# Ordered first transfers, first combinations made from a second load of x, and more projections placed behind the two norms in one decoder step

## The chip, the cores and the metric

The kernel runs on one core of a Trainium2 chip. The metric is the device time of one execution in microseconds (us). Five engines work side by side, each with its own queue of instructions: TensorE (PE; it holds a 128x128 block of weights and streams columns past it), VectorE (DVE), ScalarE (ACT), GpSimd (POOL) and SyncE (SP). SP, ACT and POOL also issue DMA transfers, which wait in the issuing engine's queue like any other instruction. Tables of times count from the start of the profiled span.

## The reference, cut to what matters

One layer of a hybrid decoder, for 1024 prompt tokens and 8 sample tokens (T = 1032) of width D = 1024:

```python
def swiglu(x, w1, w3, w2):                 # w1, w3: 1024 x 2816, w2: 2816 x 1024
    return (silu(x @ w1) * (x @ w3)) @ w2

x = layer_norm(ALPHA * x + 0.5 * swiglu(x, ffn1_w1, ffn1_w3, ffn1_w2), ln1_g, ln1_b)
m, states = hybrid_mixer(x, ...)           # RG-LRU branch + gated delta rule (8 heads)
x = layer_norm(ALPHA * x + m, ln2_g, ln2_b)
x = layer_norm(ALPHA * x + 0.5 * swiglu(x, ffn2_w1, ffn2_w3, ffn2_w2), ln3_g, ln3_b)

def hybrid_mixer(x, ...):
    rg_x, rg_y, q, k, v, z, gdn_a, gdn_b, gate_a, gate_b = split(x @ w_in + b_in)
    # RG-LRU: causal conv (4 taps) of rg_x, two block gates, a scan over time
    # gated delta: q, k, v through a causal conv and silu; beta = sigmoid(gdn_b),
    # g = -exp(a_log) * softplus(gdn_a + dt_bias); chunks of tokens with a
    # triangular solve per chunk and a state that is carried from chunk to chunk
    return merged @ w_o, new_state
```

Everything is fp32; the new states of the sample tokens are outputs too.

## The kernel before, in words

**Precision.** Each fp32 operand of a matmul is split in a high and a low part (`split`, L86 to L89 and L91 as the profile names them: a copy on ACT, then a subtraction on DVE). `mm3` multiplies high by high, high by low and low by high, so one projection of 128 output columns for one chunk of tokens is 8 x 3 = 24 matmuls of 128x344. `XH`, `XL` hold the two parts of the layer's input for all tokens, `wh`, `wl` (four buffers each) the two parts of half a weight block (four blocks of 128x128). A weight block first lands in one of three buffers `wraw`.

**Chunks.** The tokens are in three chunks of 344 (`ts(t)`), called c0, c1, c2 here. Each layer norm works by chunk: a sum over the columns, subtraction of the mean, a sum of squares, the scale (`mu`, `rs`), then eight pairs of `ACC`, `XH`, `XL`. The subtractions for `XL` of three of the eight row blocks are on POOL.

**A feed-forward layer** (`ffn`, n = 1 and 2) has 22 units `f` of 128 hidden columns. A *plain* unit is 144 matmuls of 128x344: for each chunk `p1` (w1) and `p3` (w3), then silu and product (`lnq`), stored to DRAM as `gs`. A *Strassen* unit does the same with seven products instead of eight, 168 matmuls of 128x258; it needs the *combinations* `CH`, `CL` of the input, which `combos` makes once in each layer: 16 sums `XH + XL` of 128x516 on POOL (into buffers `G`, `u2`, `si`), 16 additions on DVE, 16 splits (ACT, then DVE). In both layers units f = 0 and 1 are plain, f = 2 to 20 are Strassen, and the combinations are made during f = 1. Unit 21 and w2 follow. In layer 2 the last steps of the norm before it (`fin`) are called from f = 0, and `states` (16 jobs for the sample tokens' states: each loads `s0` and `rb` on POOL's queue, scales on ACT, adds on DVE and stores from ACT's queue, in three steps) is stepped from the units.

**Start.** Unit 0 of layer 1 loads its own x: c0 in eight pieces `ACC<-x` on ACT's queue, c1 and c2 on SP's queue among the weights; the scheduler of the program settled the order in each queue. Constants are loaded on POOL's queue.

**The mixer's beginning** (`kqv_first`): projections K and Q of head 0, `kq(t, i)`, placed around the last steps of LN1; `ab(t)`, 16 matmuls that give the gates' inputs; transposes (L707, L708), the gates' chain of some 25 small operations on DVE that ends with `GG` and `BETA`; and V of head 0, 72 matmuls. Then `gdn(0)` starts from `GG`: factors `gu` on POOL, `kt`, `lt`, a triangular solve `X` of 28 steps on DVE, two passages through DRAM (`d<-lt`, `BL<-d`, and `d<-X`, `IC<-d`), then the matmuls of L848. Projections of the RG branch (`ps_mm` from `wh`, all L130) are placed between these by the scheduler, which sets a fixed order on each engine when the program is built.

## Time and profile before

| what | value |
|---|---|
| time, median of 3 runs | 2636.21 us (2635.96 to 2637.09) |
| the profiled execution | 2637.03 us |
| its span | 2635.1 us |
| granted TensorE clock, mean | 0.984 |
| PE busy | 2535.4 us (96%) |
| DVE busy | 1784.2 us (68%) |
| ACT busy | 1133.9 us (43%) |
| POOL busy | 493.8 us (19%) |

The profiled execution took 1.9 us more than its span and 0.8 us more than the median of the runs. In the tables by window each row gives the stretch, its length, the busy time and count of PE, PEld (the weight loads), DVE, ACT and POOL, the granted clock (1.00 is full), the share of the DMA engines and GB/s. In the timeline a row gives start, length, engine, line, operation, output and inputs, the count, and in brackets the idle time of the engine before it and what ended it. ACTq and SPq are the DMA instructions in those engines' queues.

### The profile page before, as it was taken

To read this page: it belongs to the slowest core of one execution; us is meant where nothing else is said; L and a number is where in the kernel's file an instruction comes from. 1 tells how busy PE (TensorE), PEld (TensorE's weight loads), DVE (VectorE), ACT (ScalarE), POOL (GpSimd) and SP (SyncE) were. 2 spreads that over 40 slices of the span, in tenths; PEclk is the share of its full clock that TensorE was granted. 3 is DMA by queue.
4 is the path that set the end of the run, shared out by engine and by line. 5 is a ranking of instruction groups with operands and counts; after the bars stand their busy time and mean duration, and the time that the engine had idled before them with its cause. 6 is when DMAs were issued, how large, how long until landed. Compare 5 with 4: busy or idle time off the path is not lost.

```text
span 2635.1 us, 47251 instructions
## 1 busy us (share of the span) xinstructions
PE 2535.4 (96%) x18398; PEld 2486.9 (94%) x18398; DVE 1784.2 (68%) x3657; ACT 1133.9 (43%) x2419; POOL 493.8 (19%) x612
## 2 busy tenths in 40 slices
PE   7999999999989999999999999999699999999996
PEld 7999999999979999999999999989699999999996
DVE  7766665645589676777767686767786666666446
ACT  4433333312363737465564637634533333332125
POOL 5000000300332021111112021144521111021013
PEclk8999999999989999999999999999899999999998
DMA  4222222423101121111211121123314444333221
GB/s 140 78 77 82 80 76 70 125 79 113 41 26 51 34 56 43 39 48 34 57 37 53 34 56 36 52 87 117 83 66 112 118 123 119 93 112 110 81 69 65
DMA packets 146816, 195.98 MB, mean 74 GB/s; under 512 B 34720, under 2 KB 75680, under 8 KB 146592
## 3 DMA queue, kind: packets, MB, share of 16 engines
q1 hardware_dynamic: 125024, 154.13, 19.3%
q0 software_dynamic: 10160, 32.06, 4.7%
q10 hardware_dynamic: 11408, 6.77, 0.9%
q8 instruction: 145, 2.38, 0.4%
q14 instruction: 79, 0.65, 0.1%
HBM read 156.15 MB, written 36.76 MB: 73 GB/s over the span
## 4 chain that ended last, share of the span: by engine, by line
PE 80%; DVE 9%; ACT 7%; issue 2%; POOL 1%; DMA 1%; ACTq 0%; SPq 0%; POOLq 0%; DVEq 0%
PE ps_mm L130 32%; PE ps_g L130 11%; PE ps_g L287 10%; PE ps_mm L287 10%; PE ps_sq L287 8%; ACT L88 2%; DVE ACC L94 2%; PE ps_g L848 2%; PE ps_sq L734 2%; DVE ACC L91 1%; ACT lnq L88 1%; DVE wl L91 1%; PE ps_g L734 1%; PE ps_g L740 1%; DMA ACC<-x 1%
## 5 line engine op out<-in xcount | busy, mean ns | idle before, releaser
L130 PE MATMUL ps_mm<-XH,wh 128*128 128x344 f32 x1680 | 568.9, 339 | 11.0 <-ACT XH L88 7.0
L130 PE MATMUL ps_mm<-XL,wh 128*128 128x344 f32 x1680 | 542.2, 323 | 6.2 <-POOL XL L91 6.1
L130 PE MATMUL ps_mm<-XH,wl 128*128 128x344 f32 x1680 | 542.7, 323 | 4.6 <-DVE wl L91 4.6
L88 ACT ACTIVATE wh<-wraw 128x512 fp32r<-128x512 f32 (+2 forms) x366 | 217.8, 599 | 423.2 <-PE ps_mm L130 155.4
L130 PEld LDWEIGHTS ps_mm<-XH,wh 128*128 128x128 f32 x1680 | 320.6, 191 | 15.3 <-ACT XH L88 7.6
L130 PEld LDWEIGHTS ps_mm<-XL,wh 128*128 128x128 f32 x1680 | 320.7, 191 | 8.9 <-POOL XL L91 6.9
L130 PEld LDWEIGHTS ps_mm<-XH,wl 128*128 128x128 f32 x1680 | 320.0, 190 | 5.7 <-DVE wl L91 5.6
L91 DVE TENSOR_TENSOR wl<-wraw,wh 128x512 fp32r<-128x512 f32 (+3 forms) x345 | 246.4, 718 | 52.5 <-ACT wh L88 47.4
L287 PE MATMUL ps_g<-CH,wh 128*128 128x258 f32 x760 | 214.7, 283 | 0.0
L287 PE MATMUL ps_g<-CH,wl 128*128 128x258 f32 x760 | 214.6, 282 | 0.0
L287 PE MATMUL ps_g<-CL,wh 128*128 128x258 f32 x760 | 214.3, 282 | 0.0
L88 ACT ACTIVATE wh<-S 128x512 fp32r<-128x512 f32 x152 | 95.8, 631 | 201.0 <-PE ps_sq L287 129.3
L287 PE MATMUL ps_mm<-XH,wl 128*128 128x258 f32 x608 | 171.5, 282 | 0.7 <-DVE wl L91 0.7
L287 PE MATMUL ps_mm<-XH,wh 128*128 128x258 f32 x608 | 171.8, 282 | 0.5 <-ACT wh L88 0.5
L287 PE MATMUL ps_mm<-XL,wh 128*128 128x258 f32 x608 | 171.3, 282 | 0.0
L342 POOL DMA_DIRECT2D gs<-G x76 | 41.5, 546 | 666.1 <-DVE G L91 618.9
L91 DVE TENSOR_TENSOR wl<-S,wh 128x512 fp32r<-128x512 f32 x152 | 105.0, 691 | 69.4 <-ACT wh L88 69.0
L287 PEld LDWEIGHTS ps_g<-CL,wh 128*128 128x128 f32 x760 | 143.5, 189 | 0.0
L287 PEld LDWEIGHTS ps_g<-CH,wh 128*128 128x128 f32 x760 | 143.2, 188 | 0.0
L287 PEld LDWEIGHTS ps_g<-CH,wl 128*128 128x128 f32 x760 | 143.1, 188 | 0.0
L88 ACT ACT_TABLE_LOAD x109 | 139.8, 1283 | 6.1 <-issue 3.3
L130 PE MATMUL ps_g<-gl,wh 128*128 128x344 f32 x444 | 142.1, 320 | 0.0
(503 smaller groups left out, 6872.5 us busy)
## 6 DMA issues: line engine op xcount, KB each, us to landing
wraw<-w SPq DMA_DIRECT2D x164, 256.0 KB, 2.8
wraw<-w_in SPq DMA_DIRECT2D x128, 256.0 KB, 2.6
gr<-gs SPq DMA_DIRECT2D x84, 258.0 KB, 2.8
gs<-G POOLq DMA_DIRECT2D x76, 258.0 KB, 2.6
wr<-w SPq DMA_DIRECT2D x76, 256.0 KB, 2.6
wraw<-w_o SPq DMA_DIRECT2D x40, 256.0 KB, 2.7
y<-ACC SPq DMA_DIRECT2D x32, 129.0 KB, 1.9
d<-lt SPq DMA_DIRECT2D x8, 512.0 KB, 3.3
```

The costliest lines, as they stand in the source:

```text
L88: return S.activation(out, in_, f, **kw)
L91: return (eng or V).tensor_tensor(out, a, b, op=op)
L94: return V.scalar_tensor_tensor(out, a, s, b, op0=op0, op1=op1)
L130: PE.matmul(p, a, b, start=(n == 0), stop=(n == 3 * nk - 1))
L287: PE.matmul(ps_[c], a[:, k, :], b, start=(start and n == 0), stop=(n == 11), skip_group_check=not start)
L342: G.dma_start(gs[f][:, s], x)
L734: x = PE.matmul(ck(p, i), a, b, start=True, stop=True)
L740: x = PE.transpose(ck(p, i), a, IDT)
L848: pin(PE.matmul(o[r, c, :], a(c), b(c), start=True, stop=True))
```

## The change

It has five parts.

1. *Start.* The pieces of x c0 are issued first, alternately on ACT's and POOL's queue; the four weight blocks of f = 0 are the first four on SP's queue, where w3's go into buffers `wr`, so that they need no free `wraw`; all loads of c1 and c2 follow in one row. These are fixed in this order.
2. *Combinations of layer 1.* The 16 sums on POOL are replaced by 16 loads of the same part of x from DRAM, on SP's queue for half of them and on POOL's for the rest.
3. *V of head 0* is held in four tiles (`hM`, `hP`, `hLT`, `hP2`; names `wv`) and computed for c0 and c1 before `ab(0)`, and for c2 after `kq(2, 1)`, ahead of the transposes.
4. *Layer 2* has three plain units, one Strassen unit less. Order: f = 0 for c0, c1; f = 1 for c0, c1, with its w1 held in other buffers (`rb`, `s0`, `wr`, `S`; names `w1rb` and so on); f = 0 for c2; f = 1 for c2; f = 2 whole; Strassen from f = 3.
5. *`states`* is stepped in layer 2 from the Strassen units alone; what is left is done behind them.

```diff
@@ -25 +25 @@
 LN_EPS = 1e-5
 RMS_EPS = 1e-6
 NF = 22
-FIRST, LASTF = 2, 21
+FIRST, LASTF = {1: 2, 2: 3}, 21
 GROUPS = [[21, 0, 1], [2, 3, 4], [5, 6, 7, 8], [9, 10, 11, 12], [13, 14, 15, 16], [17, 18, 19, 20]]
 TH_ = T // 2
 TQ = T // 4
@@ -105 +105 @@
 
     LNB = {"s1": 3, "mu": 1, "s2": 2, "lnq": 3}
 
-    def wload(src, nk, m=128, eng=None, hold=None):
+    def wload(src, nk, m=128, eng=None, hold=None, raws=None, pin=False):
         hl = []
         for k0 in range(0, nk, 4):
             n = min(4, nk - k0)
             pad = [128, 512 // m, m]
-            raw = wp.tile([128, n, m], F32, name="wraw", tag="wraw", bufs=3, padded_shape=pad)
+            raw = raws() if raws else wp.tile([128, n, m], F32, name="wraw", tag="wraw", bufs=3, padded_shape=pad)
             if hold:
                 h, l = hold(n)
             else:
                 h = wp.tile([128, n, m], F32R, name="wh", tag="wh", bufs=4, padded_shape=pad)
                 l = wp.tile([128, n, m], F32R, name="wl", tag="wl", bufs=4, padded_shape=pad)
-            nc.sync.dma_start(raw, src[:, k0:k0 + n])
+            x = nc.sync.dma_start(raw, src[:, k0:k0 + n])
+            if pin:
+                tc.keep_in_program_order(x)
             split(h, l, raw, eng)
             hl += [(h[:, k, :], l[:, k, :]) for k in range(n)]
         return hl
@@ -140 +142 @@
 
     def x_load(t):
         for k in range(KD):
-            (nc.sync if t else nc.scalar).dma_start(ACC[:, k, ts(t)], A["x"][:, k, ts(t)])
+            q = nc.sync if t else (nc.scalar, G)[k % 2]
+            tc.keep_in_program_order(q.dma_start(ACC[:, k, ts(t)], A["x"][:, k, ts(t)]))
+
+    def x_split(t):
+        for k in range(KD):
             split(XH[:, k, ts(t)], XL[:, k, ts(t)], ACC[:, k, ts(t)])
 
     exps = []
@@ -232 +238 @@
         split(h, l, raw)
         return h, l
 
-    def combos(up):
+    def combos(up, x_src):
         CH_ = up.tile([128, 4, 4, TH_], F32R, name="CH")
         CL = big.tile([128, 4, 4, TH_], F32R, name="CL", tag="A")
         yield CH_, CL
@@ -244 +250 @@
             x1a, x1b, x2a, x2b = b
             for x, r, h in ((x2b, k + 4, 1), (x1b, k, 1), (x1a, k, 0), (x2a, k + 4, 0)):
                 c = slice(h * TH_, (h + 1) * TH_)
-                tt(x, XH[:, r, c].bitcast(F32), XL[:, r, c].bitcast(F32), OP.add, G)
+                if x_src is not None:
+                    d = (nc.sync if k < 2 else G).dma_start(x, x_src[:, r, c])
+                    if k < 2:
+                        tc.keep_in_program_order(d)
+                else:
+                    tt(x, XH[:, r, c].bitcast(F32), XL[:, r, c].bitcast(F32), OP.add, G)
             tt(x2b, x2b, x1b, OP.subtract)
             tt(x1b, x1a, x1b, OP.subtract)
             stt(x1a, x2b, -1.0, x1a, OP.mult, OP.subtract)
@@ -341 +352 @@
         def store(f, s, x):
             G.dma_start(gs[f][:, s], x)
 
-        def plain(f, put, after=None):
-            a1 = wload(w1[f], KD)
-            if n == 1 and f == 0:
+        def weights(f, hold=None, raws=None):
+            first = n == 1 and f == 0
+            if first:
                 x_load(0)
-            a3 = wload(w3[f], KD)
-            for t in range(NT):
+            a1 = wload(w1[f], KD, hold=hold, pin=first)
+            if first:
+                x_split(0)
+            return a1, wload(w3[f], KD, hold=hold, raws=raws if first else None, pin=first)
+
+        def plain(f, put, after=None, w=None, chunks=range(NT), raws=None):
+            a1, a3 = w or weights(f, raws=raws)
+            for t in chunks:
                 s = ts(t)
                 if n == 1 and f == 0 and t:
                     x_load(t)
+                    x_split(t)
                 p1 = psum("mm")
                 mm3(p1[:, :TC], a1, xsl(t), KD)
                 if fin and f == 0 and t < 2:
@@ -365 +383 @@
 
         with pool("ffna%d" % n) as up:
             extra = side(up)
-            make = combos(up)
+            make = combos(up, A["x"] if n == 1 else None)
+            spare = ["S"] * 3 + ["wr"] * 3 + ["s0", "rb"]
+
+            def held(n):
+                return [up.tile([128, n, 128], F32R, name="w1" + x, tag=x, bufs=3 if x in ("S", "wr") else 2) for x in (spare.pop(), spare.pop())]
             for f in range(LASTF):
-                if f < FIRST:
-                    def put(s, p1, p3):
+                if f < FIRST[n]:
+                    def put(s, p1, p3, f=f):
                         si = third()
                         act(si, p1, AF.Silu)
                         stt(si, si, -1.0, p3, OP.mult, OP.mult)
@@ -381 +403 @@
                         if f or t == NT - 1:
                             next(make, None)
                     cx = None if f == 0 else cx
-                    plain(f, put, after)
+                    if n == 1 or f > 1:
+                        plain(f, put, after, raws=lambda: up.tile([128, 4, 128], F32, name="wr", tag="wr", bufs=3))
+                    elif f == 0:
+                        first = (weights(0), put)
+                        plain(0, put, None, first[0], range(2))
+                    else:
+                        w = weights(1, hold=held)
+                        plain(1, put, None, w, range(2))
+                        plain(0, first[1], None, first[0], range(2, NT))
+                        cx = next(make)
+                        next(make)
+                        plain(1, put, None, w, range(2, NT))
+                        next(make)
                 else:
                     strassen(f, w1, w3, up, cx, store)
                     for _ in range(NT):
                         next(extra, None)
+            for _ in extra:
+                pass
 
         with pool("ffnb%d" % n) as up:
             ACC = big.tile([128, KD, T], F32, name="ACC", tag="A")
...
@@ -587 +623 @@
             def ck(x, c):
                 return x[:, c * 128:(c + 1) * 128]
 
-            def pre_tile():
-                pre = mp.tile([128, 3 + T], F32, name="pre", tag="pre", bufs=2)
+            def pre_tile(tag="pre"):
+                pre = mp.tile([128, 3 + T], F32, name="pre", tag=tag, bufs=2 if tag == "pre" else 1)
                 G.memset(pre[:, :3], 0.0)
                 return pre
 
@@ -646 +682 @@
 
             def kqv_first():
                 dst = kqv_dst(0)
+                spare = ["hM", "hP", "hLT", "hP2"]
+
+                def hold(n):
+                    return [mp.tile([128, n, 128], F32R, name="wv", tag=spare.pop()) for _ in range(2)]
                 wk, wq = (wload(A["w_in"][b0], KD) for b0 in (KC, QC))
-                evs = [silu_evac(d, pre_tile(), b0) for d, b0 in zip(dst, (KC, QC))]
+                wv = wload(A["w_in"][VC], KD, hold=hold)
+                evs = [silu_evac(d, pre_tile(x), b0) for d, b0, x in zip(dst, (KC, QC, VC), ("pre", "pre", "lt"))]
                 ab = gates_proj()
 
                 def kq(t, i):
                     p = psum("mm")
-                    mm3(p[:, :TC], (wk, wq)[i], xsl(t), KD)
+                    mm3(p[:, :TC], (wk, wq, wv)[i], xsl(t), KD)
                     evs[i][1](t, p[:, :TC])
 
                 kq(0, 0)
@@ -662 +703 @@
                 next(fin)
                 next(fin)
                 kq(1, 1)
+                kq(0, 2)
+                kq(1, 2)
                 ab(0)
                 ab(1)
                 ab(2)
                 kq(2, 0)
                 kq(2, 1)
+                kq(2, 2)
                 gates()
                 for t in range(NT):
                     for e in evs:
                         e[2](t)
-                for _ in proj(VC, silu_evac(dst[2], pre_tile(), VC)[0]):
-                    pass
                 KQV[0] = dst
 
             GG = mp.tile([128, 9, H], F32, name="GG")
...
```

What this does to the engines' queues, at three places. SP's queue from its first instruction, before (`w_1` stands for w1 and w3 of layer 1):

```order
L119 DMA wraw<-w_1 128x512 x3
L143 DMA ACC<-x 128x344 x6
L119 DMA wraw<-w_1 128x512
L143 DMA ACC<-x 128x344 x10
L119 DMA wraw<-w_1 128x512 x3
L261 DMA wr<-w_1 128x512 x3
L119 DMA wraw<-w_1 128x512
```

and after:

```order
L119 DMA wraw<-w_1 128x512 x2
L119 DMA wr<-w_1 128x512 x2
L146 DMA ACC<-x 128x344 x16
L254 DMA G<-x 128x516 x4
L119 DMA wraw<-w_1 128x512 x3
L272 DMA wr<-w_1 128x512 x3
L119 DMA wraw<-w_1 128x512
L254 DMA si<-x 128x516
L254 DMA u_468<-x 128x516
L254 DMA u_467<-x 128x516
L254 DMA si<-x 128x516
L272 DMA wraw<-w_1 128x512 x3
```

All 16 loads of c1 and c2, and four loads of x for the combinations, now stand between the weights of f = 0 and those of f = 1; the last two weights of f = 0 no longer stand behind six and sixteen pieces of x.

POOL's queue from the first store of f = 0, before:

```order
L342 DMA gs<-lnq 128x344
L91 ISA
L91 TENSOR_TENSOR u_468<-XH,XL 128x516
L342 DMA gs<-lnq 128x344
L91 TENSOR_TENSOR G<-XH,XL 128x516 x4
L91 TENSOR_TENSOR si<-XH,XL 128x516
L91 TENSOR_TENSOR u_467<-XH,XL 128x516
L91 TENSOR_TENSOR si<-XH,XL 128x516
L91 TENSOR_TENSOR G<-XH,XL 128x516 x3
L342 DMA gs<-lnq 128x344
```

and after:

```order
L353 DMA gs<-lnq 128x344
L254 DMA G<-x 128x516 x3
L353 DMA gs<-lnq 128x344
L254 DMA G<-x 128x516
L353 DMA gs<-lnq 128x344
L254 DMA si<-x 128x516
L254 DMA u_616<-x 128x516
L254 DMA u_615<-x 128x516
L254 DMA si<-x 128x516
```

The additions are gone from POOL; eight loads of x stand between the stores, so that the fourth load waits for the second chunk's product and the next four for the third's.

PE around the gates of head 0. Before, this is where `GG` is first used:

```order
L130 MATMUL ps_mm_8728<-XH_69,wl_8718 128x344
L130 MATMUL ps_mm_8728<-XH_69,wh_8717 128x344
L130 MATMUL ps_mm_8728<-XL_70,wh_8717 128x344
L724 MATMUL ps_g_8532<-GG_8167,masks_82 128x64 x2
L724 MATMUL ps_g_8532<-GG_8167,ONES_72 128x64
L130 MATMUL ps_mm_8728<-XH_69,wl_8718 128x344
L130 MATMUL ps_mm_8728<-XH_69,wh_8717 128x344
L130 MATMUL ps_mm_8728<-XL_70,wh_8717 128x344
L130 MATMUL ps_mm_8728<-XH_69,wl_8718 128x344
L740 MATMUL ps_g_8738<-masks_82,kq0_8173 128x128 x4
```

and after:

```order
L132 MATMUL ps_mm_8844<-XL_70,wh_8723 128x344
L132 MATMUL ps_mm_8844<-XH_69,wl_8724 128x344
L132 MATMUL ps_mm_8844<-XH_69,wh_8723 128x344
L766 MATMUL ps_g_8624<-GG_8167,masks_82 128x64 x2
L766 MATMUL ps_g_8624<-GG_8167,ONES_72 128x64
L782 MATMUL ps_g_8738<-masks_82,kq0_8173 128x128 x4
L782 MATMUL ps_g_8761<-masks_82,kq0_8173 128x128 x4
L810 MATMUL ps_g_8796<-gu_8706,SLR_83 128x512
L810 MATMUL ps_g_8796<-gu_8707,SLR_83 128x512
L132 MATMUL ps_mm_8844<-XL_70,wh_8723 128x344
```

Row for row, 72 matmuls of V and 70 more of the RG branch now stand ahead of the first use of `GG`, where before there were 77 between the transposes and it. In both programs PE has the same matmuls up to some 220 rows behind this place, and from there to the end of the mixer the same rows in the same order.

DVE in layer 2, where the weights of the first plain unit behind the norm's last chunk are split (`wl`). Before, these are f = 1's:

```order
L94 SCALAR_TENSOR_TENSOR lnq_21009<-lnq_21009,ps_g_20984 128x344
L91 TENSOR_TENSOR G_21072<-G_21072,G_21070 128x516
L91 TENSOR_TENSOR wl_21091<-wraw_21089,wh_21090 128x512
L91 TENSOR_TENSOR G_21070<-G_21069,G_21070 128x516
L91 TENSOR_TENSOR CL_21068<-G_21072,CH_21067 128x516
L94 SCALAR_TENSOR_TENSOR G_21069<-G_21072,G_21069 128x516
L91 TENSOR_TENSOR wl_21097<-wraw_21095,wh_21096 128x512
```

and after, they are f = 2's:

```order
L91 TENSOR_TENSOR CL_21200<-si_21277,CH_21199 128x516
L91 TENSOR_TENSOR G_21374<-G_21373,G_21374 128x516
L91 TENSOR_TENSOR CL_21200<-G_21376,CH_21199 128x516
L91 TENSOR_TENSOR wl_21297<-wraw_21295,wh_21296 128x512
L94 SCALAR_TENSOR_TENSOR G_21373<-G_21376,G_21373 128x516
L91 TENSOR_TENSOR CL_21200<-G_21374,CH_21199 128x516
L91 TENSOR_TENSOR wl_21303<-wraw_21301,wh_21302 128x512
L94 SCALAR_TENSOR_TENSOR G_21375<-G_21373,G_21375 128x516
L91 TENSOR_TENSOR CL_21200<-G_21373,CH_21199 128x516
L91 TENSOR_TENSOR wl_21309<-wraw_21307,wh_21308 128x512
L91 TENSOR_TENSOR CL_21200<-G_21375,CH_21199 128x516
```

Before, one operation of the combinations stood ahead of the first of these; now 18 stand between the norm's last `XL` and it.

More of the change, by code (lines that the diff above doesn't have):

```diff
@@ L569, in full @@
             def full(tag, n=T):
-                return mp.tile([128, n], F32, name=tag, tag=tag, padded_shape=[128, T])
+                return mp.tile([128, n], F32, name=tag, tag=tag, padded_shape=[128, 3 + T if tag == "lt" else T])
             def eight(tag):
@@ L1067, in slots @@
                             x = mp.tile([128, n * TC], F32R, name="m_" + tag, tag=tag, bufs=2 if tag == "pre" else 1,
-                                        padded_shape=[128, 512] if tag[0] == "h" else [128, TC] if n == 1 else [128, 3 + T] if tag == "pre" else [128, T])
+                                        padded_shape=[128, 512] if tag[0] == "h" else [128, TC] if n == 1 else [128, 3 + T] if tag in ("pre", "lt") else [128, T])
                             ap += [x[:, i * TC:(i + 1) * TC] for i in range(n)]
```

## The prediction

> **What bounds the kernel now.** I read the page first, then PE's busy time by stretch, then PE's waits in the three stretches that the change touches, and there the other engines' timeline.
>
> ```profile
> span 2635.1 us, 47251 instructions
> PE 2535.4 (96%) x18398; PEld 2486.9 (94%) x18398; DVE 1784.2 (68%) x3657; ACT 1133.9 (43%) x2419; POOL 493.8 (19%) x612
> ...
> PE 80%; DVE 9%; ACT 7%; issue 2%; POOL 1%; DMA 1%; ACTq 0%; SPq 0%; POOLq 0%; DVEq 0%
> ```
>
> PE is the bound, 80% of the chain that ended last, and the rest is DVE and ACT at a few places. The windows show where:
>
> ```profile
> core 0: us, PE busy (x) PEld busy (x) DVE busy (x) ACT busy (x) POOL busy (x), PEclk, DMA share, GB/s
> ...
> 6.54:23.52 16.98, 12.80 (x48) 11.01 (x49) 8.51 (x19) 9.22 (x20) 1.19 (x3) 0.80 1.01 317
> 23.52:38.59 15.07, 15.07 (x98) 15.07 (x97) 10.61 (x14) 8.53 (x21) 11.22 (x8) 1.00 0.17 65
> 38.59:73.60 35.01, 27.99 (x149) 26.93 (x147) 34.91 (x41) 12.80 (x23) 18.98 (x14) 0.85 0.15 46
> 73.60:93.61 20.01, 20.01 (x166) 20.01 (x167) 15.70 (x41) 8.20 (x18) 1.08 (x2) 1.00 0.29 91
> 741.85:787.46 45.61, 37.79 (x197) 31.73 (x196) 37.75 (x67) 29.17 (x57) 12.82 (x15) 0.85 0.07 24
> 787.46:800.34 12.88, 12.88 (x88) 12.66 (x87) 12.06 (x43) 5.45 (x13) 1.05 (x3) 1.00 0.14 42
> 800.34:843.41 43.07, 43.07 (x291) 42.58 (x290) 39.59 (x102) 18.86 (x62) 15.42 (x19) 1.00 0.23 61
> 1863.67:1944.39 80.72, 57.51 (x292) 54.18 (x293) 70.40 (x88) 39.28 (x71) 42.55 (x37) 0.85 0.22 60
> 1944.39:1964.61 20.22, 20.22 (x170) 20.22 (x169) 14.44 (x27) 6.67 (x13) 1.08 (x2) 1.00 0.27 90
> ```
>
> The second row is layer 1's f = 0 for c1 and c2: 96 matmuls of 128x344 in 15.07 us, 0.157 us each, so 24 take 3.77 us and a plain unit 22.6 us. The last row is a Strassen unit, 20.2 us. The first row is f = 0 for c0: 48 matmuls in 16.98 us that need 7.5. The third is f = 1 and two matmuls of the first Strassen unit: 35.0 us for about 23. In layer 2, f = 0 and 1 take 80.7 us for 45.2. Once a Strassen unit has begun, PE is busy throughout, so each of these stretches shifts everything behind it one for one. The mixer is different, as below.
>
> **The start.**
>
> ```profile
> PE ps_mm L130 <- ACT XH L88: 7.0, 2, 6.5
> PE ps_g L130 <- ACT wh L88: 3.6, 1, 3.6
> PE ps_mm L130 <- DVE wl L91: 3.0, 1, 3.0
> PE ps_g L130 <- DVE wl L91: 2.8, 1, 2.8
> ```
>
> ```profile
> 9.86 0.49 ACT L88 ACTIVATE XH<-ACC 128x344 fp32r<-128x344 f32 x1 [0.51 <-DMA ACC<-x]
> 11.34 3.05 ACTq L143 DMA_DIRECT2D ACC<-x  x3
> 14.43 1.20 ACT L88 ACTIVATE wh<-wraw 128x512 fp32r<-128x512 f32 x2 [4.08 <-DMA ACC<-x]
> ```
>
> ```profile
> GB/s 0 0 41 141 344 402 372 345 362 392 357 288 192 183 88 255 388 397 393 377 378 387 374 343 360 268 266 306 331 341 284 371 361 156 146 119 11 22 0 0
> ```
>
> ACT issues five pieces of c0, and the last three only at 11.34 to 14.39; `wh` of w3 stands behind them, and PE waits 3.6 us for it. The row of GB/s (40 slices of the first 30 us) stands near 370 with a hole around 10 us. After, four weight blocks and eight pieces of x, 4 x 256 KB + 8 x 172 KB = 2.46 MB, are first in all queues: at 370 GB/s 6.6 us, from about 3.0, landing by 10 to 11. ACT then has XH's last pieces and w3's `wh` done near 11.6; p3 of c0 starts near 12 and c0 ends at 16 (estimates from these rows). Bounds: 14 (PE's 7.5 us right behind the first pieces) and 20.5 (only the 3.05 us saved). I take 16.5, since no issue now stands between. Then 15.1 us for c1 and c2; their 2.82 MB need 7.6 us more, so they are in by 19, ahead of PE.
>
> For the combinations, DVE and POOL disturb each other:
>
> ```profile
> 32.74 5.06 POOL L91 TENSOR_TENSOR G<-XH,XL 128x516 f32<-128x516 f32 x4
> 33.64 8.41 DVE L91 TENSOR_TENSOR wl<-wraw,wh 128x512 fp32r<-128x512 f32 x1 [1.80 <-ACT wh L88]
> ```
>
> One `wl` took 8.41 us, its wait through seven POOL sums of 1.27 us each; this is PE's 3.0 us, the 2.8 behind it is the same again, and the clock of 0.85 is the rest. After, there are no POOL sums here. PE comes to f = 1 at 16.5 + 15.1 = 31.6. By then DVE has 24 `XL`, the first four sums and their splits; counted off in its order, f = 1's four `wl` are ready at about 29, 31, 34 and 36, needed at 31.6, 33.5, 35.4 and 37.3. That is tight: the second half of G waits for c1's store on POOL's queue. I leave 3 us of stalls (bounds 0 and 6, what the two waits took). f = 3 then starts at 31.6 + 22.6 + 20.2 + 3 = 77.4 instead of 93.6: **-16 us** (-21 to -10). The 4.2 MB that x is loaded again fall into stretches in which DMA moved 65 and 46 GB/s, so they displace little.
>
> A rule speaks against the first part. The Trainium skill ("Trainium Kernel Development and Optimization", Key Constraints) says that transfers from SP, ACT and POOL share the same 16 engines, and that issuing from several saves only issue time. The trace agrees on the shared rate (370 to 400 GB/s, whichever queues run); by the rule alone only the 3.05 us of issue would go. That is the bound of 20.5 above.
>
> **LN1 and V.**
>
> ```profile
> PE ps_mm L699 <- DVE XL L94: 2.9, 2, 2.2
> PE ps_sq L169 <- DVE s L91: 2.6, 1, 2.6
> ```
>
> V's c0 and c1 (48 matmuls, 7.5 us) cover the 2.9 us wait of `ab(2)`, and most of the slow clock (0.85 of 45.6 us is 6.8 us of lost work). But V's 11.3 us now stand ahead of the transposes: 787.5 + 11.3 less about 9.5 (the wait and most of the clock's loss) = 789.3. What counts is this chain:
>
> ```profile
> 788.21 0.29 DVE L91 TENSOR_TENSOR GT<-ps_g,b_ab 128x128 f32<-128x128 f32 x1 [0.61 <-PE ps_g L708]
> ...
> 800.05 0.22 DVE L94 SCALAR_TENSOR_TENSOR GG<-GG,a_log 128x72 f32<-128x72 f32 x1
> ...
> 838.30 0.37 DVE L808 COPY X<-X 32x256 f32<-32x256 f32 x1
> ...
> 840.78 0.67 SPq L816 DMA_DIRECT2D IC<-d  x1
> ...
> 843.41 0.64 PE L848 MATMUL ps_g<-IC,hLT 128*64 128x16 f32 x8
> ```
>
> From the transposes to `GG` it takes 12 us and from there to `IC` 43 us, with DVE busy 39.6 of 43.1 (window). PE arrives at L848 just when `IC` is there, and from some rows behind this its order is the same in both programs. So the 9 us or so that PE saves at LN1 only become waits in the first 40 us of `gdn(0)`, unless DVE's chain starts earlier or is shorter. It starts 2 us later, and carries about 3 us less of other work (counted in the orders: 46.6 for 49.5 us). I take **-1 us**, -4 if DVE's waits shrink too, +4 if the chain is not shortened and the clock drops.
>
> **Layer 2.**
>
> ```profile
> PE ps_sq L169 <- DVE s L91: 6.7, 1, 6.7
> PE ps_mm L130 <- POOL XL L91: 6.1, 3, 3.2
> PE ps_mm L130 <- ACT wh L88: 4.0, 1, 4.0
> PE ps_g L130 <- DVE wl L91: 3.8, 1, 3.8
> ```
>
> ```profile
> 1881.25 0.40 ACT L88 ACTIVATE s<-s,KE 128x128 f32<-128x128 f32 x1 [4.15 <-DMA s<-S]
> ...
> 1893.70 0.49 ACT L88 ACTIVATE mu<-mu 128x344 f32<-128x344 f32 x1
> ```
>
> ```profile
> 1908.80 5.28 DVE L91 TENSOR_TENSOR G<-G 128x516 f32<-128x516 f32 x1
> ...
> 1918.55 2.97 DVE L91 TENSOR_TENSOR CL<-G,CH 128x516 fp32r<-128x516 f32 x3
> 1921.44 3.44 DVE L91 TENSOR_TENSOR wl<-wraw,wh 128x512 fp32r<-128x512 f32 x2
> ```
>
> The wait of 4.0 stays. The 6.7 us end late because `states` holds ACT's queue until a load of S lands (1881.25), ahead of the mean; with the job moved down, two weight copies stand there instead. I take 2 us earlier (0 to 5): scale ready at 1892.2 instead of 1894.2. From there PE has 2.7 us of c1's p3, then f = 1 for c0, c1 (15.1), f = 0 c2 and f = 1 c2 (15.1): f = 2 at 32.9 behind the scale. The last `XL` comes about 20 behind it (15.5 before, three more POOL sums ahead), needed at 21: the 6.1 us go. What is late next is f = 2's `wl`, behind 18 operations of the combinations: DVE's own work of 10.3 for the norm and 18 x 0.6 to 1.0 (last rows) is 21 to 28, and POOL's ten sums and four `XL` of together 16 us can block it (the 5.28 us). Between 25 and 38 I take 35, nearer the upper, since here both engines are loaded at once; the last `wl` at 44, where PE wants it at 38.6. Stall 5.5 us (0 to 10). f = 2 is 22.6 us, and f = 3 starts at 1892.2 + 32.9 + 5.5 + 22.6 = 1953.2 instead of 1964.6: **-11 us** (-17 to -5). In it is that a plain unit costs 2.4 us more than the Strassen unit it replaces. `states` needs some 52 steps, 18 Strassen units give 54.
>
> **Sum.** -16 - 1 - 11 = -28 against the profiled execution's 2637.0: 2609; that stands 0.8 us above the median, so 2608.
>
> **Rivals.**
> 1. *The weights of the unit behind the combinations are late in both layers*: stalls of 6 and 10 us instead of 3 and 5.5. For it speaks that DVE is 34.9 of 35.0 us busy in f = 1 before; against it that in layer 1 POOL is free. 2608 + 7.5, about 2616. Chance 0.25.
> 2. *The start saves issue time only* (the rule above): c0 ends at 20.5; 2612, and with rival 1, 2620. 0.15.
> 3. *The mixer takes the whole gain of LN1.* If `gdn(0)` has slack that I do not see, 8 us more go: 2600. Against it, DVE's 92%. 0.12.
> 4. *Slower:* the jobs of `states`, all in Strassen units now, hold ACT's queue as at 1881.25. If a unit's `wh` copies stood 4.15 us behind each of 16 jobs and half of it reached PE, that is +33 us, 2641; it decides from 1.8 us for each job on. Against it: in before's Strassen units the same jobs run and PE is busy for all of 20.2 us. 0.03.
> 5. *No difference to measure* (5.3 us, 0.2%, is about the least that can be told from no change): all three terms at their upper bounds and a little more. 0.04.
>
> My forecast has 0.41. The range of 8 in 10 goes from rival 3 with a little more, 2598, to rivals 1 and 2 together, 2622. Faster by over 0.2%: 0.92; same 0.05; slower 0.03.
>
> **What would show it.** Right: the first Strassen matmul (L298) near 57 us; no DVE operation above 2 us between 15 and 55; ps_mm <- XL no longer in LN1's waits, but new PE waits between 790 and 845 (shifted by 16) ahead of `IC`; in layer 2 `wl` as PE's longest wait behind the norm. Wrong: PE waits for x or wraw at f = 1; `IC` more than 4 us off; ACT waiting for `s<-S` in Strassen units.

## The result, and the profile after

The changed kernel takes 2612.01 us (median of 4 runs, 2609.49 to 2612.86), the kernel before on the same chip 2636.65 us (2635.96 to 2637.68). The ratio is 0.9902, with an interval from 0.9887 to 0.9918: 24.6 us less, where 28 were forecast. Line numbers have moved: L132 is the matmul of `mm3` (L130 before), L298 Strassen's (L287), L175 the sums of the layer norm (L169), L890 the matmuls that wait for `IC` (L848).

The head of the page, and the shares of the chain that ended last:

```profile
span 2611.0 us, 47192 instructions
...
PE 2529.6 (97%) x18374; PEld 2484.1 (95%) x18374; DVE 1749.7 (67%) x3641; ACT 1129.4 (43%) x2414; POOL 477.6 (18%) x609
...
PE 83%; ACT 7%; DVE 6%; POOL 1%; issue 1%; DMA 1%; ACTq 0%; SPq 0%; DVEq 0%; POOLq 0%
```

PE has 83% of that chain instead of 80, DVE 6 instead of 9. The windows, cut at the same places of the program as before (c0, c1 and c2 of f = 0, f = 1, a Strassen unit; LN1's last sums to the transposes, to `GG`, to `IC`; layer 2's f = 0 and 1, f = 2, a Strassen unit):

```profile
5.63:17.35 11.72, 11.72 (x48) 10.52 (x49) 8.59 (x18) 9.37 (x21) 3.82 (x8) 1.00 1.04 346
17.35:32.42 15.07, 15.07 (x98) 15.07 (x97) 13.17 (x26) 11.71 (x26) 3.23 (x6) 1.00 0.95 326
32.42:55.04 22.62, 22.62 (x147) 22.62 (x145) 19.41 (x33) 10.56 (x19) 3.77 (x7) 1.00 0.53 177
55.04:75.20 20.16, 20.16 (x169) 20.16 (x169) 13.80 (x37) 7.53 (x16) 1.08 (x2) 1.00 0.21 64
723.44:772.41 48.97, 44.51 (x269) 40.95 (x267) 46.58 (x85) 33.52 (x65) 14.82 (x18) 0.97 0.12 39
772.41:784.17 11.76, 11.76 (x81) 11.70 (x81) 11.13 (x40) 4.79 (x11) 0.29 (x2) 1.00 0.01 1
784.17:827.85 43.68, 39.60 (x251) 37.80 (x250) 34.77 (x97) 17.22 (x59) 12.41 (x19) 0.96 0.22 59
1845.95:1909.53 63.58, 51.72 (x292) 50.05 (x292) 49.91 (x64) 31.55 (x57) 40.72 (x31) 0.89 0.18 50
1909.53:1940.67 31.14, 25.62 (x145) 25.34 (x145) 22.33 (x36) 11.77 (x23) 7.82 (x10) 0.89 0.42 121
1940.67:1960.88 20.21, 20.21 (x170) 20.21 (x170) 12.31 (x22) 5.74 (x11) 1.08 (x2) 1.00 0.21 66
```

In the first four rows PE is busy throughout, and from the second on at the full clock; f = 1 takes 22.6 us, 35.0 before. The 1.00 of the first row is not a reading: the trace has no entry of the clock before 13.4 us. Its 48 matmuls take 11.7 us where 7.5 are needed, because they start 0.29 us apart or more up to 13.2 us, and 0.157 apart behind it. One of each:

```profile
12.59 0.49 PE L132 MATMUL ps_mm<-XH,wl 128*128 128x344 f32 x1
13.74 0.32 PE L132 MATMUL ps_g<-XL,wh 128*128 128x344 f32 x1
```

Ahead of the transposes PE is idle for 4.5 us (48.97 less 44.51), and between `GG` and `IC` for 4.1, where before it was idle for 7.8 and 0. In layer 2, f = 2 takes 31.1 us for 22.6 us of work.

At four places that both programs pass, the trace gives the three terms (starts in the trace, us):

| place | before | after | difference | so this part |
|---|---|---|---|---|
| second Strassen unit of layer 1, f = 3 | 93.61 | 75.20 | -18.4 | start -18.4 |
| first use of head 1's `IC` | 961.81 | 944.42 | -17.4 | mixer +1.0 |
| f = 3 of layer 2 | 1964.61 | 1940.67 | -23.9 | layer 2 -6.5 |
| last matmul | 2624.13 | 2599.90 | -24.2 | the rest -0.3 |

### The profile page after: what moved, and what is told of

It reads as the page before. It is cut to its first block, busy times and chain, and to the rows that moved or that the text cites. A ratio compares the mean times of both kernels' runs of the same rounds, so it can differ in the third digit from the quotient of the medians.

```text
span 2611.0 us, 47192 instructions
## 1 busy us (share of the span) xinstructions
PE 2529.6 (97%) x18374; PEld 2484.1 (95%) x18374; DVE 1749.7 (67%) x3641; ACT 1129.4 (43%) x2414; POOL 477.6 (18%) x609
## 4 chain that ended last, share of the span: by engine, by line
PE 83%; ACT 7%; DVE 6%; POOL 1%; issue 1%; DMA 1%; ACTq 0%; SPq 0%; DVEq 0%; POOLq 0%
PE ps_mm L132 34%; PE ps_g L132 12%; PE ps_g L298 10%; PE ps_mm L298 10%; PE ps_sq L298 8%; ACT L88 2%; PE ps_g L890 2%; DVE ACC L94 2%; PE ps_sq L776 2%; ACT lnq L88 1%; POOL s L91 1%; PE ps_g L776 1%; PE ps_g L782 1%; DVE ACC L91 1%; ACT ACC L88 1%
## 5 line engine op out<-in xcount | busy, mean ns | idle before, releaser
L132 PE MATMUL ps_mm<-XH,wh 128*128 128x344 f32 x1656 | 560.8, 339 | 12.4 <-ACT wh L88 12.4
L132 PE MATMUL ps_mm<-XH,wl 128*128 128x344 f32 x1656 | 535.6, 323 | 3.7 <-DVE wl L91 3.7
L132 PE MATMUL ps_mm<-XL,wh 128*128 128x344 f32 x1656 | 534.5, 323 | 0.0
L132 PEld LDWEIGHTS ps_mm<-XH,wh 128*128 128x128 f32 x1656 | 316.2, 191 | 16.2 <-ACT wh L88 12.9
L132 PEld LDWEIGHTS ps_mm<-XH,wl 128*128 128x128 f32 x1656 | 315.5, 190 | 4.9 <-DVE wl L91 4.6
L132 PEld LDWEIGHTS ps_mm<-XL,wh 128*128 128x128 f32 x1656 | 316.3, 191 | 1.6 <-DVE XL L91 0.6
L91 DVE TENSOR_TENSOR wl<-wraw,wh 128x512 fp32r<-128x512 f32 (+3 forms) x339 | 228.9, 679 | 42.3 <-ACT wh L88 38.2
L298 PE MATMUL ps_g<-CH,wh 128*128 128x258 f32 x740 | 209.0, 282 | 0.0
L298 PE MATMUL ps_g<-CH,wl 128*128 128x258 f32 x740 | 208.9, 282 | 0.0
L298 PE MATMUL ps_g<-CL,wh 128*128 128x258 f32 x740 | 208.7, 282 | 0.0
L298 PE MATMUL ps_mm<-XH,wh 128*128 128x258 f32 x592 | 167.1, 282 | 0.0
L298 PE MATMUL ps_mm<-XH,wl 128*128 128x258 f32 x592 | 166.9, 282 | 0.0
L298 PE MATMUL ps_mm<-XL,wh 128*128 128x258 f32 x592 | 166.8, 282 | 0.0
L132 PE MATMUL ps_g<-gl,wh 128*128 128x344 f32 x444 | 142.1, 320 | 0.0
L132 PE MATMUL ps_mm<-gl,wh 128*128 128x344 f32 x444 | 142.1, 320 | 0.0
L132 PE MATMUL ps_g<-gh,wh 128*128 128x344 f32 x444 | 142.0, 320 | 0.0
L132 PE MATMUL ps_mm<-gh,wh 128*128 128x344 f32 x444 | 142.0, 320 | 0.0
```

The costliest lines, as they stand in the source:

```text
L91: return (eng or V).tensor_tensor(out, a, b, op=op)
L132: PE.matmul(p, a, b, start=(n == 0), stop=(n == 3 * nk - 1))
L298: PE.matmul(ps_[c], a[:, k, :], b, start=(start and n == 0), stop=(n == 11), skip_group_check=not start)
```

## The experiments

Every kernel here is timed against the kernel before on the same chip (2636.9 to 2637.7 us there).

**The start alone.** The changed kernel without parts 2 to 5: POOL's sums stay, V is computed behind the transposes, layer 2 has two plain units in their old order.

```diff
-FIRST, LASTF = {1: 2, 2: 3}, 21
+FIRST, LASTF = {1: 2, 2: 2}, 21
...
-            make = combos(up, A["x"] if n == 1 else None)
+            make = combos(up, None)
...
```

> Part 1 alone (order of the first transfers). If the terms are independent: c0 ends 6.2 us earlier, f = 1 keeps its two waits of 3.0 and 2.8 us and its slow clock, 2636.7 - 6.2 = 2630.5. Rival: the waits in f = 1 end when POOL's sums end, at a time that the start does not move; then f = 1 only waits longer and the gain is 0 to 3 us, 2634 to 2637.

2630.98 us (2629.09 to 2632.08), ratio 0.9974 [0.9963, 0.9985]. c0 ends at 16.98 us instead of 23.52, 6.5 us earlier, but f = 3 only 5.15 us. PE's waits in the first 75 us, and the window of f = 1, of this kernel:

```profile
PE ps_mm L132 <- ACT wh L88: 10.3, 2, 5.6
PE ps_mm L132 <- DVE wl L91: 5.2, 1, 5.2
```

```profile
33.00:68.00 35.00, 25.81 (x143) 25.31 (x144) 33.86 (x43) 14.03 (x25) 15.33 (x13) 0.80 0.19 66
```

The 5.6 us are the first matmul's. The rest, 9.9 us, stands in f = 1, where PE was idle for 7.0 us in the kernel before: its stalls did not go, and they grew by about 3 us.

**The combinations alone.** The kernel before, with the sums on POOL replaced by loads of x in layer 1.

```diff
-                tt(x, XH[:, r, c].bitcast(F32), XL[:, r, c].bitcast(F32), OP.add, G)
+                if x_src is not None:
+                    d = (nc.sync if k < 2 else G).dma_start(x, x_src[:, r, c])
+                else:
+                    tt(x, XH[:, r, c].bitcast(F32), XL[:, r, c].bitcast(F32), OP.add, G)
...
```

> Part 2 alone (x loaded again in place of POOL's sums, with the start as before). If the contention of POOL's sums with DVE is the whole cause of the losses in f = 1: no DVE operation above 2 us, no PE wait in f = 1, 12.2 us less, 2624.5. Rival: the loads, behind 24 pieces of x and on POOL's queue behind the stores, come later than the sums were; PE waits for wl by 3 us or more, and the gain is 6 us or less, 2631 or more.

2624.12 us (2623.23 to 2625.85), ratio 0.9945 [0.9929, 0.9962]. f = 3 comes at 82.17 us, 11.4 earlier, and the window in f = 1 has no idle PE:

```profile
40.00:62.00 22.00, 22.00 (x143) 22.00 (x141) 16.48 (x28) 9.06 (x16) 2.70 (x5) 1.00 0.37 124
```

**Both.** The changed kernel with layer 2 and the mixer as in the first experiment (the same edit of `FIRST`, V back behind the transposes).

> Parts 1 and 2 (start and combinations of layer 1) without parts 3, 4 and 5. If the parts add up, as the landmarks of the two traces say: the first Strassen unit's steady part 18.4 us earlier than before and nothing else, 2636.7 - 18.4 = 2618. If a later stretch gives part of it back (the mixer's chain, DMA at LN1), 2621 or more.

2617.87 us (2615.61 to 2618.81), ratio 0.9921 [0.9907, 0.9936]. 6.1 and 13.0 us alone, 19.3 together: the two add up.

**c0 on one queue.** The eight pieces of c0 all on ACT's queue; nothing else differs from the changed kernel.

```diff
-            q = nc.sync if t else (nc.scalar, G)[k % 2]
+            q = nc.sync if t else nc.scalar
```

> The changed kernel with all eight pieces of c0 issued on ACT's queue, none on POOL's. If the order of issue is what counts and the queues share the same engines: c0 ends within 1 us of the changed kernel (17.35 us), later by at most the issue time of four more pieces on ACT (4 x 0.45 = 1.8 us). If POOL's queue gives bandwidth of its own: c0 ends 3 us or more later. The whole 2612 to 2614.

2619.28 us (2614.84 to 2622.07), ratio 0.9934 [0.9918, 0.9951]. c0 ends at 23.03 us, 5.7 later than in the changed kernel and only 0.5 ahead of the kernel before; 1 to 1.8 later was expected. The whole is 7.3 us slower in the median, but its runs spread over 7 us, and the profiled one is only 2.0 slower than the changed kernel's. The timeline of ACT from its start, first of the changed kernel, then of this one:

```profile
0.74 1.85 ACTq L146 DMA_DIRECT2D ACC<-x  x4
```

```profile
0.73 7.14 ACTq L146 DMA_DIRECT2D ACC<-x  x8
7.91 1.28 ACT L88 ACT_TABLE_LOAD   x1 [7.91 <-DMA wr<-w]
```

Four pieces take ACT 1.85 us to issue, eight take 7.14. In the trace pieces 6, 7 and 8 are issued at 4.23, 5.39 and 7.54 us, each just behind the landing of an earlier transfer: with SP's weights, eight transfers of SP and ACT were on their way each time. Counted from the end of the issue to the landing, SP and ACT together never have more than eight on their way in any trace of this study, and POOL's queue reaches eight of its own beside them. The last piece lands at 13.64 us instead of 10.53, and ACT's copies to `XH` stand behind the issues. PE's first matmul, in the changed kernel and in this one:

```profile
PE ps_mm L132 <- ACT wh L88: 5.6, 1, 5.6
```

```profile
PE ps_mm L132 <- ACT XH L88: 10.8, 1, 10.8
```

It begins 5.2 us later, which is nearly all of the 5.7.

**The mixer without V.** The changed kernel without part 3.

```diff
-                kq(0, 2)
-                kq(1, 2)
...
-                kq(2, 2)
                 gates()
...
+                for _ in proj(VC, silu_evac(dst[2], pre_tile(), VC)[0]):
+                    pass
```

> The changed kernel without part 3 (V again behind the gates). If the chain on DVE from the transposes to IC bounds gdn(0): L890 1.0 to 1.1 us earlier against the start of LN1 and the whole 1 us faster than the changed kernel, 2611. If V's cover is worth what it removes of PE's waits at LN1 (2.9 us and the slow clock, 8 us in all): 2620.

2610.66 us (2609.86 to 2611.25), ratio 0.9895 [0.988, 0.991]: without V ahead of the transposes the kernel is, if anything, a microsecond faster. Part 3, as it stands, brought nothing.

**V's last chunk behind the transposes.**

```diff
-                kq(2, 2)
                 gates()
+                kq(2, 2)
```

> The changed kernel with V's third chunk (24 matmuls, 3.8 us) behind the gates' transposes instead of ahead. If DVE's chain from the transposes to IC bounds: the transposes 3.8 us earlier, IC 2.5 to 3.5 us earlier, the whole about 3 us faster than the changed kernel, 2609. If PE's own work bounds the beginning of gdn(0): nothing, 2612.

2606.14 us (2604.2 to 2607.03), ratio 0.988 [0.9865, 0.9895]: 6 us less than the changed kernel, where 3 were expected. The windows of this kernel, from the sums of c2 to the transposes, to `GG` and to `IC`:

```profile
723.60:767.34 43.74, 40.78 (x244) 37.31 (x243) 42.73 (x78) 31.82 (x62) 17.76 (x16) 0.96 0.10 30
767.34:779.87 12.53, 12.53 (x85) 12.20 (x84) 11.96 (x43) 4.51 (x12) 1.57 (x4) 1.00 0.16 49
779.87:820.73 40.86, 36.99 (x245) 35.45 (x245) 36.55 (x97) 17.60 (x60) 13.01 (x18) 1.00 0.21 53
```

The transposes begin 5.1 us earlier (767.34 for 772.41), `IC` is used 7.1 earlier, and 6.2 are left at the second head (938.23 for 944.42). From `GG` to `IC` it now takes 40.9 us for 43.7. Against the kernel without part 3 this is 4.5 us less: V for c0 and c1 is worth something ahead of the transposes, V for c2 is not.

**The jobs of `states` in other buffers.** In the changed kernel f = 1's eight held tiles leave one of two `rb` and one of two `s0` free, and the first job of `states` can load into these at once. Here they take both of each, so that its loads go out only behind f = 1.

```diff
-            spare = ["S"] * 3 + ["wr"] * 3 + ["s0", "rb"]
+            spare = ["S"] * 2 + ["wr"] * 2 + ["s0"] * 2 + ["rb"] * 2
```

> The changed kernel with f = 1's w1 and w3 of layer 2 held in both buffers of s0 and of rb (and one S and one wr less), so that the first load of the states' jobs comes behind f = 1. If the jam of those two loads with the weights (7.6 us to landing instead of 2.5) delays the mean of LN2: w1wr's copy and the mean 5 us earlier, the wait of 7.0 us falls to 2, the first Strassen unit of layer 2 comes 5 us earlier, 2607. If the weights are slow for another reason, or the wait has another cause: 2612. A loss is possible if the later loads jam the Strassen weights.

2608.11 us (2605.96 to 2611.33), ratio 0.9889 [0.9875, 0.9904]. PE's waits from the norm to f = 2's end, and what ACT does ahead of the mean, in the changed kernel:

```profile
PE ps_sq L175 <- DVE s L91: 7.0, 1, 7.0
PE ps_mm L132 <- ACT wh L88: 6.7, 2, 4.0
PE ps_mm L132 <- DVE wl L91: 3.7, 2, 2.8
```

```profile
1856.30 0.63 ACT L88 ACTIVATE w1rb<-wraw 128x512 fp32r<-128x512 f32 x1
1862.43 0.63 ACT L88 ACTIVATE w1wr<-wraw 128x512 fp32r<-128x512 f32 x1 [5.50 <-DMA wraw<-w]
1862.97 0.44 ACT L88 ACTIVATE mu<-ps_sq 128x344 f32<-128x344 f32 x1
```

and in this one (of the waits only that for the sums):

```profile
PE ps_sq L175 <- DVE s L91: 2.0, 1, 2.0
```

```profile
1856.21 0.63 ACT L88 ACTIVATE w1s<-wraw 128x512 fp32r<-128x512 f32 x1 [0.43 <-DMA wraw<-w]
1857.32 0.46 ACT L88 ACTIVATE mu<-ps_sq 128x344 f32<-128x344 f32 x1 [0.47 <-PE ps_sq L175]
```

In the changed kernel a weight of f = 1 was issued at 1854.83 and landed at 1862.41, 7.6 us, beside `rb` (broadcast from `rtd`) and `s`, which landed at 1862.06 and 1863.22; the two weights before it took 2.5. ACT stood at its copy with the mean queued behind. Without that jam the mean follows the sums at once, and the first Strassen unit begins at 1933.80 us instead of 1940.67; 0.8 us of this lie ahead of layer 2.

**f = 2's weights ahead of the second quarter of the combinations.**

```diff
                         next(make)
+                        w2_ = weights(2, spin=True)
                         plain(1, put, None, w, range(2, NT))
```

`spin` fixes the splits of these weights, and the next operations of the combinations behind them, in the order in which they are written.

> The changed kernel with f = 2's weights of layer 2 split ahead of the second quarter of the combinations, on ACT and DVE. If f = 2 waits only for its place behind the combinations: the two waits (2.7 and 2.8 us) and the slow clock behind them go, f = 2 takes 22.6 us instead of 31.1, the whole 8 us faster, 2604. Rival: the combinations then are late themselves and the first Strassen unit waits for CL; the gain is 0 to 3 us.

2617.21 us (2613.09 to 2621.07), ratio 0.9923 [0.9908, 0.9937]: slower than the changed kernel. PE's two longest waits behind f = 2, in the first Strassen unit (L303 is Strassen's matmul here):

```profile
PE ps_mm L303 <- ACT wh L88: 5.4, 1, 5.4
PE ps_mm L303 <- DVE wl L91: 2.4, 1, 2.4
```

f = 2's stalls are gone (it ends at 1930.7 us, 10 us earlier), and as much is lost one unit later: these 7.8 us, and a slower clock behind them. f = 4 begins at 1961.70 us, 1960.88 in the changed kernel. That accounts for no gain. The profiled execution is 2.5 us slower than the changed kernel's, and the four runs spread over 8 us; why the median is 5 us slower is not settled.

**Two plain units in layer 2**, in the changed kernel's interleaved order.

```diff
-FIRST, LASTF = {1: 2, 2: 3}, 21
+FIRST, LASTF = {1: 2, 2: 2}, 21
...
-                        next(make)
+                        for _ in make:
+                            pass
```

> The changed kernel with two plain units in layer 2 again, in the new order (f = 0 and f = 1 interleaved, Strassen from f = 2). If the combinations on DVE and POOL bound this stretch (their last CL came at 1926 in the changed kernel, PE was through with f = 1 at 1909.5): the first Strassen unit waits for CL until about 1926, f = 3 starts at 1943 to 1946 instead of 1940.7, the whole 3 to 5 us slower than the changed kernel, 2615 to 2617. If the third plain unit only costs its 2.4 us: 2609.6.

2623.68 us (2620.18 to 2625.97), ratio 0.9945 [0.993, 0.996]: 11.7 us slower than with three, where 3 to 5 were expected, though a Strassen unit is 2.4 us shorter. The first Strassen unit waits, for its weights and not for `CL`:

```profile
PE ps_mm L298 <- DVE wl L91: 11.2, 1, 11.2
PE ps_g L298 <- ACT wh L88: 4.0, 1, 4.0
PE ps_mm L298 <- ACT wh L88: 3.1, 1, 3.1
```

**Layer 2's combinations without POOL.** Is it the number of DVE's operations, or POOL's sums that hold them up?

```diff
-            make = combos(up, A["x"] if n == 1 else None)
+            make = combos(up, A["x"])
```

> The changed kernel, but layer 2's combinations are made from loads of x too, instead of POOL's 16 sums of XH and XL. Part of the computation is changed: they are made of the program's input x and not of LN2's output, so only the time is read. Theory (POOL's sums hold up DVE, whose operations take 1.0 to 1.2 us instead of 0.69 in this stretch, and so f = 2's weights are late): DVE's operations on CL and G go back to about 0.69 us, the two waits of 2.8 and 2.7 us in f = 2 go and f = 2 takes 22.6 us instead of 31.1; the first Strassen matmul of layer 2 comes 8 to 10 us earlier, the time is 2602 to 2604. Rival (DVE has too many operations there, POOL or not): DVE's operations are shorter, but f = 2 still waits 3 us or more for wl, and the time falls by at most 3 us, 2609 or more.

2604.86 us (2604.47 to 2605.2), ratio 0.988 [0.9865, 0.9895]. DVE's splits of one group of the combinations in 1876 to 1941 us, first of the changed kernel, then of this one (count, busy time in us, mean in ns):

```profile
L91 DVE TENSOR_TENSOR CL<-G,CH 128x516 fp32r<-128x516 f32 x8 | 8.5, 1095 | 0.0
```

```profile
L91 DVE TENSOR_TENSOR CL<-G,CH 128x516 fp32r<-128x516 f32 x8 | 5.2, 684 | 0.0
```

And the windows from LN2's last sums to f = 3, in the same order:

```profile
1872.76:1940.67 67.91, 62.39 (x363) 61.35 (x363) 53.12 (x68) 28.74 (x51) 36.09 (x30) 0.92 0.23 68
```

```profile
1872.96:1932.18 59.22, 59.22 (x363) 58.74 (x363) 39.47 (x68) 27.71 (x51) 14.28 (x22) 0.96 0.36 113
```

The same 363 matmuls take 8.7 us less, without any idle PE; as many operations of DVE, 68, take 39.5 us instead of 53.1. It was POOL's sums. Two things change with them, though. DVE's operations are shorter, and the loads, of the program's x in place of LN2's output, wait for nothing in the norm (what layer 2 computes is changed): six operations of the combinations, 4 us of DVE, ran ahead of LN2's scale here (1872.8 to 1877.0). f = 2's first `wl` came 16.1 us earlier (1898.79 for 1914.89), so the head start is the smaller part by this count, but no run separates the two. In layer 1 too the loads need no `XH` and `XL`.

**The same with two plain units.**

> The changed kernel with two plain units in layer 2 instead of three, in the same interleaved order, and layer 2's combinations made from loads of x (of the program's input, not of LN2's output: part of the computation is changed, and only the time is read). With POOL's sums this variant took 2623.7 and its first Strassen unit waited 11.2 us for wl. Theory (POOL's sums hold up DVE): without them two plain units are enough, as they are in layer 1; the 11.2 us go, and the time is 2600 to 2606. Rival (DVE's own operations and the norm don't fit in two units): the first Strassen unit still waits 5 us or more, 2612 to 2620.

2612.41 us (2610.81 to 2615.59), ratio 0.9907 [0.989, 0.9923]. Against 2623.68 with POOL's sums this is 11.3 us less, and the 11.2 us for `wl` are gone; a wait of 5.4 for `wh` is left in the first Strassen unit, and the time falls in the rival's range, but not for the rival's reason. The timeline of ACT:

```profile
1909.15 0.46 ACT L88 ACTIVATE lnq<-ps_mm 128x344 f32<-128x344 f32 x1 [1.49 <-PE ps_mm L132]
1917.43 0.98 ACT L88 ACTIVATE s<-s,KE 128x128 f32<-128x128 f32 x3 [7.82 <-DMA s<-S]
1920.46 0.63 ACT L88 ACTIVATE wh<-S 128x512 fp32r<-128x512 f32 x1 [2.04 <-DVE S L91]
```

ACT is not loaded but waits at the first job of `states`, whose load of S was issued beside the unit's own weights (`rb` took 7.3 us, S 8.4, three weights 7.3 to 8.3). These weights landed at 1916.3 to 1918.4 us, so by these times `wh` could have come little earlier without the job's own wait: what counts is that all of them landed late.

**V late and the jobs late**: the two edits above that gained, together.

> Both of the last two runs' gains together: V's third chunk behind the transposes, and the states' first loads behind f = 1 of layer 2. If they add up: 6 us at gdn(0) and 5 us at LN2 less than the changed kernel, 2601. If one takes the other's gain (LN2's wait is set by something that comes with the mixer): 2605 or more.

2603.07 us (2601.87 to 2605.07), ratio 0.9869 [0.9853, 0.9886]. The two gains, 5.9 and 3.9 us against the changed kernel, come to 8.9 together. This is the fastest kernel of the study.

## Why the prediction came out right

Direction, bound and place were right. That the sum came within 3.4 us is partly luck: the start gave 2.4 us more than forecast, which made up a third of what the mixer (2.0) and layer 2 (4.9) fell short. By its steps:

- **The start** (-16 forecast, -18.4 measured). The two halves were each shown alone. c0 ended at 17.35, forecast 16.5; the lower bound of 14 was out of reach here, since it counts 7.5 us for 48 matmuls, of which the first 22 came 0.29 us apart or more. The term that was mis-sized is "I leave 3 us of stalls": f = 1 took 22.62 us with no wait, so f = 3 came at 75.2 and not at 77.4. The rows say why there was room. The group of f = 1's `wl` splits and one of the combinations' splits (DVE, 15 to 60 us), before and then after:

```profile
L91 DVE TENSOR_TENSOR wl<-wraw,wh 128x512 fp32r<-128x512 f32 x6 | 14.0, 2355 | 5.1 <-ACT wh L88 5.1
L91 DVE TENSOR_TENSOR CL<-G,CH 128x516 fp32r<-128x516 f32 x4 | 4.4, 1129 | 0.0
```

```profile
L91 DVE TENSOR_TENSOR CL<-G,CH 128x516 fp32r<-128x516 f32 x8 | 5.3, 689 | 0.3 <-ACT CH L88 0.3
L91 DVE TENSOR_TENSOR wl<-wraw,wh 128x512 fp32r<-128x512 f32 x6 | 4.1, 685 | 1.2 <-ACT wh L88 1.2
```

  Six splits in 4.1 us instead of 14.0, none slow: "no DVE operation above 2 us" held.
- **The rule against the start** (rival 2, c0 at 20.5) did not hold as it was used: it priced the issue at 3.05 us. The Trainium skill ("Trainium Kernel Development and Optimization", Key Constraints) has several queues save issue time only. c0 from ACT's queue alone was 5.7 us later than from two. The bandwidth is shared, as it says (346 GB/s in c0's window from three queues); but the issue itself waits for earlier transfers, and holds the engine that has to split what has landed.
- **The mixer** (-1 forecast, +1.0 measured). That PE's gain at LN1 turns into waits ahead of `IC` was right: the wait of 2.9 us for `XL` went, the one for the sums stayed, and PE has new ones, here in 700 to 846 us:

```profile
PE ps_sq L175 <- DVE s L91: 5.7, 3, 2.5
PE ps_sq L175 <- ACT wh L88: 3.0, 1, 3.0
PE ps_g L776 <- DVE kt L91: 1.9, 1, 1.9
PE ps_g L810 <- POOL gu L91: 1.1, 3, 0.5
PE ps_g L890 <- DMA IC<-d: 1.1, 1, 1.1
```

  The last three, 4.1 us, are PE's idle time between `GG` and `IC`. Two steps were off. The transposes came 3.4 us later by the start's clock (772.41 + 18.41 = 790.8 against 787.5), forecast 2. And "the chain carries about 3 us less" did not shorten it: 43.7 us from `GG` to `IC`, 43.1 before, though DVE's busy time there fell from 39.6 to 34.8 (from the transposes to `GG` it was 1.1 us shorter). The chain looks like a row of steps that wait for one another, so that work taken out from between them leaves idle time; no run tests this. The +1.0 itself is not clear of chance: from f = 3 of layer 1 to head 1's `IC` the seven profiled kernels with all of V ahead take 868.4 to 872.4 us, the five with V behind 866.5 to 868.5. The two with only V's last chunk behind, 862.9 and 864.0, are clear of both. Rival 3 named the right place for more (2600), but by the wrong mechanism: what was to be had, 6 us, needed the transposes early, not PE's gain.
- **Layer 2** (-11.4 forecast, -6.5 measured): 4.9 us off, in two steps. "The mean 2 us earlier" failed: the wait for the sums stayed, 7.0 us for 6.7, since the first loads of `states` now went out beside f = 1's weights, and ACT, which no longer stood at S, stood at a weight. (Part 5 is less than it says: in the source both kernels step layer 2's jobs in the Strassen units alone, `plain` does it only for `n == 1`, and the change adds the loop behind them. Where the first loads stand is the scheduler's choice in both.) f = 2 so began 1.8 us later than forecast (1909.53 + 17.4 = 1926.9 against 1925.1). The stall of 5.5 us was right as a wait (2.8 for `wl`, 2.7 for `wh`), but with the clock at 0.89 f = 2 lost 8.5 us in all; the price of a stall left out the slow clock that came with it, 3 us (the granted clock was 0.50 from 1914.62 to 1921.44). `wl` was the longest wait of f = 2 by 0.1 us. The two runs with loads in layer 2 show the cause: POOL's sums, which layer 1 no longer has and layer 2 still has.
- **Rival 1**, late weights in both layers, did not hold: layer 1 had no stall, and in layer 2 PE waited the 5.5 us of the forecast and not 10; with the clock's part the loss of 8.5 lies between. **Rival 4**, a slow ACT, was half there: behind f = 3 ACT does wait for S, and PE does not notice. ACT's longest wait and PE's only one, 1945 to 2330 us, changed kernel:

```profile
ACT s L88 <- DMA s<-S: 55.7, 14, 5.4
```

```profile
PE ps_sq L298 <- DVE G L91: 0.5, 1, 0.5
```

  Before, ACT's wait for S was 55.0 us in the same stretch. Only the first job, issued beside weights that are wanted at once, reached PE (5.4 us with two plain units).

## What to carry to other kernels

Where two engines slow each other, count the stretch again with one of them quiet before you reckon in single waits: 16 sums on POOL cost layer 1 some 11 us and layer 2 up to 9, more than PE's idle time in f = 1 of layer 1 (7.0) and in f = 2 of layer 2 (5.5). A projection that fills PE's idle time ahead of a long chain of dependent steps is worth nothing if it also delays the chain's first step; put what delays it behind that step. When a load is moved, look at what will be in flight beside it.

## What the hardware showed that was not expected

- **DVE and POOL.** One 128x512 subtraction on DVE took 8.41 us while seven POOL sums ran, and 0.68 without them; POOL's own sums grew too, from 1.27 us to a mean of 2.4 in one group (15 to 60 us, before):

```profile
L91 POOL TENSOR_TENSOR u<-XH,XL 128x516 f32<-128x516 f32 x3 | 7.3, 2420 | 0.1
```

  The Trainium skill ("SBUF — State Buffer", "SBUF: two separate sides") describes a pair of ports that a DVE operation with two inputs in SBUF and a GpSimd operation hold for a whole instruction, the other one waiting. The runs with loads agree that the two engines conflict (a split of 128x516 on DVE took 1095 ns with POOL's sums and 684 without); no run shows a port. A wait through seven sums is more than one holder's turn: if it is this lock, the waiting operation was passed over again and again.
- **Issue that waits.** With eight transfers of SP and ACT on their way, the next one held its engine's queue until one landed: 7.14 us for eight pieces on ACT, 1.85 for four. POOL's queue had eight of its own beside them.
- **Loads beside a broadcast.** A weight of 256 KB took 7.6 us beside the broadcast load of `rb` and a load of S, 2.5 us just before. Which of the two does it was not separated.
